# New instruction orders for five queues of a hybrid attention and DeltaNet layer, with the small float32 products of a blockwise inverse in uncut blocks

## The chip, the cores and the metric

The kernel runs on one core of a Trainium2 chip. The metric is the device time of one execution in microseconds (us). A core has five engines that matter here, each with a queue of its own that is executed in order: TensorE (PE in the profile; its weight loads are listed as PEld), VectorE (DVE), ScalarE (ACT), GpSimd (POOL) and SyncE (SP, which issues most of the DMAs). An instruction waits on semaphores of other engines; while it waits, everything behind it in its own queue waits too.

## The reference

The reference is one layer of a diffusion backbone over 512 latent tokens with 256 context tokens, model width 1024, all in float32. A token-mixing half has two branches, softmax attention (8 heads, 2 key/value heads) and a bidirectional gated DeltaNet (8 heads, chunks); their outputs are gated, merged and projected. A channel-mixing half is a gated MLP of width 2816 with a depthwise convolution. The part around which the changed order turns is the triangular solve of the DeltaNet, one unit lower triangular matrix per head, direction and chunk:

```python
a_mat = jnp.where(strict, beta[..., :, None] * dec * kk, 0.0) + jnp.eye(GDN_CHUNK)
rhs = jnp.concatenate([beta[..., None] * v, (beta * jnp.exp(gam))[..., None] * k], axis=-1)
uw = lax.linalg.triangular_solve(a_mat, rhs, left_side=True, lower=True, unit_diagonal=True)
...
delta = u_c - jnp.einsum('bhcd,bhde->bhce', w_c, s)
s_new = gl_c[..., None, None] * s + jnp.einsum('bhcd,bhce->bhde', kd_c, delta)
```

## The kernel before

**Large products.** Every large weight product is done as three products of float32r operands. A weight block of 128x1024 is loaded (`wraw`), ACT rounds it to a high part (`whi`), DVE subtracts to get the low part (`wlo`), and `mm3` multiplies high by high, high by low and low by high into one PSUM bank. In the trace these are the groups of three 128x512 matmuls `mb<-hxH,whi`, `mb<-hxL,whi`, `mb<-hxH,wlo` (the input projections), `pq` (query and key projections), `pS` and `ab` (attention), and `mc` (output projection and MLP).

**Stages.** In order of time: normalisation and modulation, query/key/value projections, attention woven with DeltaNet projections, then the DeltaNet, and from about 789 us on the output projection and the MLP. The DeltaNet goes over four pairs of heads, p = 0 to 3. Through the whole DeltaNet the queue of PE is filled up with the remaining projections (`filler()`), which depend on little, so PE has a large `mb` product at hand while a small chain of the DeltaNet goes through the other engines.

**The solve and the inverse.** Each pair has 12 matrices of 128x128 per direction, made block by block. `gdn_solve` first forms the products of keys (`pk<-kT`), DVE multiplies them into the decay (`NN`), DVE and ACT transpose the diagonal 32x32 blocks (`C`, `X`), and a chain of 31 steps on `R` (`prod`, `R`) inverts all 32x32 diagonal blocks. This chain runs on DVE for pair 0 and on POOL for pairs 1 to 3; for pair p+1 it runs while PE works on pair p. DVE then multiplies `R` by `gT` and transposes it twice, into `o_tr` and `o_nt`. `gdn_inv` assembles the inverse from there in four steps of small float32 products on PE, with copies out of PSUM between them:

1. 48 products of 32x32, `pb<-o_tr,NN` and `pb<-o_nt,NN`, copied to `Y1` by two DVE and two ACT copies;
2. 48 products of 32x32, `pb<-Y,o_nt` and `pb<-Y,o_tr`, copied into `TTm` by DVE and ACT;
3. 24 products of 64x64, `pb<-TTm,NN`, copied to `Y2_0` and `Y2_1`;
4. 24 products of 64x64, `pb<-Y,Tm` (`Y_0`, `Y_1` in the queue's rows), copied into `TTm` by ACT.

The products of a step use parts of the 128x128 array, four different 32x32 parts or two different 64x64 parts by turns, as the loop of the first step shows:

```python
for u in range(12):
    for (d, a, b), py in zip(AB, pys):
        mm(py[q(a), u, :], NN[q(b), u, q(a)], TT[d][q(b), 12 * d + u, :])
```

A float32 product is two records in the trace, a transpose and a float32r product one. After `gdn_inv` follows `gdn_scan`, six steps of 128x128 float32 products (`pb<-S,kT`, `pb<-r,TTm`, `pb<-dk,ktok` and others) that hand over to DVE and ACT in between.

**What sets the order.** All instructions are recorded by wrappers around the five engines, in the order of the program text. At the end `arrange` puts each engine's instructions into the order of a string of numbers, `V_ORDER` (DVE), `A_ORDER` (ACT), `G_ORDER` (POOL), `S_ORDER` (SP) and `T_ORDER` (PE). A number is the instruction's place in the program text, and "260-265" is a run of them. Only the places change; what waits for what follows from the data. Because the recording is a helper, nearly all instructions carry one line, L301 before and L275 after.

Of the kernel before, what the change touches and what calls it, by code (L numbers as in the profile page):

```python
# [70 lines left out]
V_ORDER = ('2 6 5 0-1 3-4 7-65 70 66 71 75 67 76-77 68 120 78 72 79-80 69 82 73 83-84 81 91 85-86 92 74 87-88 90 '  # L71
# [218 lines left out]
def hybrid_layer_body(tc, ctxt, xT, consts, cols, rows, w_mod1, w_mod2, w_av, w_aq, w_cm, w_pa, w_pd, w_out,  # L290
# [27 lines left out]
    def keep(i):  # L318
        return i if V_ORDER else tc.keep_in_program_order(i)

# [1641 lines left out]
```

## Time and profile before

| What | Value |
|---|---|
| median of 3 runs | 1210.79 us (1210.16 to 1213.17) |
| the profiled execution, its own time | 1211.39 us |
| its span | 1209.6 us |
| mean granted clock of TensorE | 0.996 |
| PE busy | 1187.7 us, 98% of the span, 7781 records |
| DVE busy | 819.9 us, 68% |
| ACT busy | 589.1 us, 49% |
| POOL busy | 254.4 us, 21% |

The table of busy time says which engine has no room; the chain of waits says what released each step. PE has under 22 us in which it does nothing, spread over the whole span, so what its instructions cost in themselves is of interest, and a busy PE can still be a PE that is slow. The timeline gives for each group of equal matmuls the start, the length and the number of records. Neighbouring matmuls overlap, so a matmul's cost is read from the step between two starts and not from its length.

### The profile page before, as it was taken

The numbers are of one execution on the slowest core, as the hardware profiler recorded it, in microseconds if no ns is written. First come the engines' busy times: TensorE is split into PE (matmuls) and PEld (weight loads), VectorE is DVE, ScalarE is ACT, GpSimd is POOL, SyncE is SP. The second block draws the span as 40 slices with busy tenths as digits, with TensorE's granted clock in tenths as the row PEclk, the third lists the DMA queues.
The fourth block names the chain that finished last, engine by engine and source line by source line (L and its number), as shares of the span: only waits on it lengthen the run. The fifth ranks groups of instructions, "written<-read, shape, count | busy, mean of one in ns | idle before, by whom it ended". The sixth has DMA issues, their size and how long they took to land.

```text
span 1209.6 us, 20365 instructions
## 1 busy us (share of the span) xinstructions
PE 1187.7 (98%) x7781; PEld 1018.6 (84%) x7781; DVE 819.9 (68%) x1614; ACT 589.1 (49%) x1372; POOL 254.4 (21%) x333
## 2 busy tenths in 40 slices
PE   9999999999998999999999999999999999999996
PEld 6899999999886887888887787889888888888886
DVE  4768788787798667857566798657767656643233
ACT  3535588776656755834535432233444434442221
POOL 0201110101324795785474111000000000000000
PEclk9999999999999999999999999999999999999999
DMA  9423233313453426345245778753432333333331
GB/s 380 161 85 117 94 106 109 103 55 133 172 204 124 153 85 212 125 130 193 93 164 198 257 244 311 238 193 105 170 126 88 105 101 100 98 93 96 96 96 70
DMA packets 57633, 174.96 MB, mean 145 GB/s; under 512 B 6240, under 2 KB 8768, under 8 KB 56128
## 3 DMA queue, kind: packets, MB, share of 16 engines
q1 hardware_dynamic: 54080, 161.08, 39.4%
q0 software_dynamic: 3456, 12.58, 3.1%
q8 instruction: 61, 1.00, 0.4%
q14 instruction: 36, 0.29, 0.1%
HBM read 146.85 MB, written 26.79 MB: 144 GB/s over the span
## 4 chain that ended last, share of the span: by engine, by line
PE 86%; DVE 6%; issue 4%; DMA 2%; ACT 1%; POOL 1%; POOLq 0%; SPq 0%; DVEq 0%; ACTq 0%
PE mc L301 34%; PE mb L301 25%; PE pb L301 8%; PE pq L301 7%; PE ab L301 5%; PE pS L301 3%; PE pm L301 1%; PE xb L301 1%; DVE R L301 1%; PE pk L301 1%; DVE wlo L301 1%; PE pt L301 1%; DVE t L301 1%; DVE prod L301 1%; DMA NN<-nnd 1%
## 5 line engine op out<-in xcount | busy, mean ns | idle before, releaser
L301 ACT ACTIVATE whi<-wraw 128x1024 fp32r<-128x1024 f32 (+3 forms) x155 | 159.4, 1031 | 204.8 <-PE mc L301 110.3
L301 DVE TENSOR_TENSOR wlo<-wraw,whi 128x1024 fp32r<-128x1024 f32 (+3 forms) x155 | 187.0, 1209 | 97.7 <-ACT whi L301 97.5
L301 PE MATMUL mc<-h,whi 128*128 128x512 f32 (+1 forms) x752 | 219.4, 376 | 0.0
L301 PE MATMUL mb<-hxH,whi 128*128 128x512 f32 x384 | 164.4, 428 | 3.3 <-DVE t L301 1.6
L301 PEld LDWEIGHTS mc<-h,whi 128*128 128x128 f32 x752 | 138.0, 188 | 25.4
L301 PE MATMUL mb<-hxH,wlo 128*128 128x512 f32 x384 | 151.9, 396 | 0.0
L301 PE MATMUL mb<-hxL,whi 128*128 128x512 f32 x384 | 150.0, 394 | 0.0
L301 PE MATMUL mc<-h,wlo 128*128 128x512 f32 (+1 forms) x376 | 141.2, 375 | 0.0
L301 PE MATMUL mc<-a,whi 128*128 128x512 f32 (+1 forms) x396 | 111.0, 366 | 0.6 <-DVE x L301 0.6
L301 POOL TENSOR_TENSOR rc<-rc,mhalf 128x2 f32<-128x2 f32 x4 | 2.8, 700 | 441.7 <-DVE rc L301 441.7
L301 PEld LDWEIGHTS mb<-hxH,whi 128*128 128x128 f32 x384 | 72.7, 189 | 18.6 <-ACT hxH L301 2.0
L301 DVE SCALAR_TENSOR_TENSOR u<-mc,col,u 128x511 f32<-128x511 f32 x88 | 64.4, 746 | 34.0 <-ACT u L301 33.3
L301 PEld LDWEIGHTS mb<-hxH,wlo 128*128 128x128 f32 x384 | 72.5, 189 | 16.3
L301 PEld LDWEIGHTS mc<-a,whi 128*128 128x128 f32 x396 | 71.6, 189 | 12.9 <-DVE x L301 0.8
L301 PEld LDWEIGHTS mc<-h,wlo 128*128 128x128 f32 x376 | 70.8, 188 | 12.9
L301 PEld LDWEIGHTS mb<-hxL,whi 128*128 128x128 f32 x384 | 72.8, 190 | 9.9 <-DVE hxL L301 0.5
L301 PE MATMUL mc<-a,wlo 128*128 128x512 f32 (+1 forms) x198 | 72.3, 365 | 0.0
L301 POOL TENSOR_TENSOR R<-R,prod 128x31 f32<-128x31 f32 (+15 forms) x93 | 57.8, 622 | 6.7
L301 POOL TENSOR_TENSOR prod<-X,R 128x31 f32<-128x31 f32 (+15 forms) x93 | 52.5, 565 | 24.3 <-DVE X L301 17.4
L301 DVE SCALAR_TENSOR_TENSOR t<-mb,col,t 128x511 f32<-128x511 f32 (+1 forms) x76 | 49.1, 646 | 12.2 <-ACT t L301 11.4
L301 PE MATMUL pq<-whi,hxH 128*128 128x256 f32 (+1 forms) x192 | 55.7, 290 | 0.0
L301 PE MATMUL pq<-wlo,hxH 128*128 128x256 f32 (+1 forms) x192 | 54.5, 284 | 0.1
(322 smaller groups left out, 2746.7 us busy)
## 6 DMA issues: line engine op xcount, KB each, us to landing
wraw<-in_w_cm_dram SPq DMA_DIRECT2D x48, 512.0 KB, 3.8
wraw<-in_w_up_dram SPq DMA_DIRECT2D x44, 512.0 KB, 3.3
wl<-in_w_mod_dram POOLq DMA_DIRECT2D x24, 512.0 KB, 4.9
wm<-in_w_mod_dram SPq DMA_DIRECT2D x8, 1024.0 KB, 13.8
wraw<-in_w_down_dram SPq DMA_DIRECT2D x16, 512.0 KB, 3.5
wraw<-in_w_aq_dram SPq DMA_DIRECT2D x10, 512.0 KB, 3.5
M<-gamdr SPq DMA_DIRECT2D x8, 512.0 KB, 6.4
wraw<-in_w_pa_dram SPq DMA_DIRECT2D x8, 512.0 KB, 3.7
```

The source lines that it names most:

```text
L301: self.made.append(fn(*a, **k))
```

## The change

The five strings are written anew; `S_ORDER` has the same numbers as before. On DVE 1171 of 1582 instructions stand at another place, on ACT 866 of 1182, on POOL 104 of 329 and on PE 4103 of 6638. The mean move is 2.0 places on DVE, 2.5 on ACT, 0.9 on POOL and 5.6 on PE; the largest is 58 places, on PE. Nothing is added, and nothing is removed: the same 6638 matmuls with the same shapes are there. The diff is the tables alone:

```diff
-T_ORDER = ('0-244 260-265 245-247 266-268 248-259 269-359 362-370 360-361 371-382 386-396 383-385 397-444 '
+T_ORDER = ('0-244 260-262 245-259 263-304 308-315 305-307 316-321 334-335 322-333 336-361 386-387 362-385 '
...
-           '2932 2936 2940 2944 2948 2952 2929 2933 2937 2941 2945 2949 2953 2930 2934 2938 2942 2946 2950 2931 '
...
+           '2920-2927 2976-2997 2928-2975 3048-3053 2998-3047 3054-3065 3070-3072 3066-3069 3085-3088 3073-3084 '
```

The small products of `gdn_inv` are the numbers that stood singly or in strides of four, as 2932, 2936, 2940; they now stand as runs in the order of the program text, as 2928-2975. Counted over the whole PE queue, a piece being a stretch of 32x32 or of 64x64 products with nothing else in between, there were 18 pieces of 32x32 products and 30 of 64x64, and now there are 8 and 9. Within the pieces a product was followed by one on the same part of the array 85 times (32x32) and 87 times (64x64); now never.

Three places show it. The first is PE in the third step of pair 1. Before:

```order
L301 MATMUL pb<-TTm,NN 64x64 x11
L301 MATMUL pk<-kT 128x128 x4
L301 MATMUL mb<-hxH,whi 128x512
L301 MATMUL mb<-hxL,whi 128x512
L301 MATMUL mb<-hxH,wlo 128x512
L301 MATMUL pb<-TTm,NN 64x64 x3
L301 MATMUL mb<-hxH,whi 128x512
L301 MATMUL mb<-hxL,whi 128x512
L301 MATMUL mb<-hxH,wlo 128x512
L301 MATMUL pb<-TTm,NN 64x64 x10
```

Now:

```order
L275 MATMUL xb<-cst,co 128x128 x4
L275 MATMUL pk<-kT 128x128 x4
L275 MATMUL pb<-TTm,NN 64x64 x24
L275 MATMUL mb<-hxH,whi 128x512
L275 MATMUL mb<-hxL,whi 128x512
L275 MATMUL mb<-hxH,wlo 128x512
```

The 24 products of the step stood in three pieces with two groups of large products and the key products of the next pair between them; they are one piece, and the key products stand ahead of it.

The second place is PE between the first and the second step of pair 1, where the second step needs the copies `Y1` of what the first one made. Before:

```order
L301 MATMUL pb<-o_nt,NN 32x32
L301 MATMUL pk<-kT 128x128 x4
L301 MATMUL pb<-o_tr,NN 32x32 x2
L301 MATMUL mb<-hxH,whi 128x512
L301 MATMUL mb<-hxL,whi 128x512
L301 MATMUL mb<-hxH,wlo 128x512
L301 MATMUL mb<-hxH,whi 128x512
L301 MATMUL mb<-hxL,whi 128x512
L301 MATMUL mb<-hxH,wlo 128x512
L301 MATMUL pb<-Y_3884,o_nt 32x32 x2
```

Now:

```order
L275 MATMUL pb<-o_tr,NN 32x32
L275 MATMUL pb<-o_nt,NN 32x32
L275 MATMUL mb<-hxH,whi 128x512
L275 MATMUL mb<-hxL,whi 128x512
L275 MATMUL mb<-hxH,wlo 128x512
L275 MATMUL mb<-hxH,whi 128x512
L275 MATMUL mb<-hxL,whi 128x512
L275 MATMUL mb<-hxH,wlo 128x512
L275 MATMUL pb<-Y_3884,o_nt 32x32
L275 MATMUL pb<-Y_3884,o_tr 32x32
```

Six large products stand between the steps in both. Before, all but the last three products of the first step stood further ahead, so most of its four banks were complete earlier; now all four banks are complete only with the end of the piece.

The third place is DVE at the same point, with the buffer numbers kept (`pb_5750` and `pb_5752` are two of the first step's four banks). Before:

```order
L301 STREAM_TRANSPOSE o_nt_5670<-R_4958 128x32x32
L301 TENSOR_TENSOR oacc_5292<-oacc_5292,pb_5693 128x2x128
L301 SCALAR_TENSOR_TENSOR t1_5618<-mb_5619,col_74,t1_5618 128x511 x2
L301 TENSOR_TENSOR wlo_6023<-wraw_6021,whi_6022 128x1024
L301 SCALAR_TENSOR_TENSOR co_5611<-co_5611,t1_5618 128x512
L301 COPY Y1_3884<-pb_5752 32x384
L301 COPY Y1_3884<-pb_5750 32x384
```

Now:

```order
L275 STREAM_TRANSPOSE o_nt_5670<-R_4958 128x32x32
L275 TENSOR_TENSOR oacc_5292<-oacc_5292,pb_5687 128x2x128
L275 STREAM_TRANSPOSE gT_6820<-g_6819 128x32
L275 TENSOR_TENSOR wlo_6023<-wraw_6021,whi_6022 128x1024
L275 COPY Y1_3884<-pb_5750 32x384
L275 TENSOR_TENSOR f_6281<-f_6281,oss_6264 128x8
L275 COPY Y1_3884<-pb_5752 32x384
```

The convolution steps `t1` and `co` have left the stretch between the transpose `o_nt` and the two copies; one weight split `wlo` still stands ahead of the copies.

More of the change, by code (lines that the diff above doesn't have):

```diff
@@ L68 @@
 AQ, AK, AM, AR = 24, 10, 32, 10
-V_ORDER = ('2 6 5 0-1 3-4 7-65 70 66 71 75 67 76-77 68 120 78 72 79-80 69 82 73 83-84 81 91 85-86 92 74 87-88 90 '
[61 rows of a table removed]
-A_ORDER = ('0-32 34 33 36-37 68 39-40 54 35 41-44 46 45 47 38 49 48 50 55 52 56-57 53 58 51 59-62 64-65 63 69-71 '
[44 rows of a table removed]
-G_ORDER = ('0-9 11 10 12-22 24 28 26 23 29 25 27 33 30 35 34 36-37 31 123 39 38 40 117 41 118 32 42 46 48 43 49 '
[4 rows of a table removed]
+V_ORDER = ('2 6 5 0-1 3-4 7-65 70 66 71 67-68 72 75-76 78 77 73 79-80 82 74 83-84 81 120 69 85 92 86 91 87 93 89 '
[61 rows of a table added]
+A_ORDER = ('0-32 34 33 36-37 68 39-40 35 41-42 54 38 43-44 46 45 47-50 55 51-53 56 58 57 60 59 61 64-65 63 62 67 '
[43 rows of a table added]
+G_ORDER = ('0-9 11-12 10 13-14 16 15 17-20 22 24 28 25-27 30 29 21 32 35 23 33 36 123 37 31 34 41 39 117-118 46 '
[4 rows of a table added]
 S_ORDER = ('0-18 21 24 22-23 25-26 19-20 27-32 34-36 38 41 33 47 54 42 44 37 39 57 40 49-50 52 63 43 45 58-59 61 '
```

366 rows, old and new, of tables (A_ORDER, G_ORDER, T_ORDER, V_ORDER) are left out of this document.

## The prediction

> **What bounds the kernel now.** I read the busy times first, then the chain of waits, then the busy times by stretches, and last the timeline of PE where the order changes. The page's busy row and chain row:
>
> ```profile
> span 1209.6 us, 20365 instructions
> PE 1187.7 (98%) x7781; PEld 1018.6 (84%) x7781; DVE 819.9 (68%) x1614; ACT 589.1 (49%) x1372; POOL 254.4 (21%) x333
> PE 86%; DVE 6%; issue 4%; DMA 2%; ACT 1%; POOL 1%; POOLq 0%; SPq 0%; DVEq 0%; ACTq 0%
> ```
>
> PE is busy for 98% of the span and holds 86% of the chain that ended last. It can get faster in two ways: by the 22 us in which it idles, or by instructions that take less of its time. Busy times by stretch (start and end, length, then the busy time of each engine with its records, the granted clock, DMA share and GB/s) show where it idles:
>
> ```profile
> 300.00:374.00 74.00, 69.56 (x395) 59.56 (x394) 63.90 (x122) 42.47 (x111) 22.42 (x16) 0.98 0.46 167
> 374.00:404.00 30.00, 30.00 (x392) 23.28 (x391) 22.19 (x35) 22.31 (x52) 10.63 (x13) 1.00 0.49 164
> 675.00:735.00 60.00, 58.10 (x355) 50.75 (x354) 52.72 (x116) 19.90 (x45) 8.08 (x16) 1.00 0.79 265
> 789.00:1190.00 401.00, 400.42 (x1949) 338.97 (x1948) 223.94 (x319) 156.84 (x225) 1.41 (x2) 1.00 0.34 111
> ```
>
> From 789 us on PE lacks 0.6 us of 401; no order of the same products can win there. In the first blockwise inverse, 374 to 404, it does not idle at all, so only the price of its instructions counts. That price is the first thing the change touches.
>
> **The price of a cut.** In the timeline (start, length, engine, operation, records), pair 1, third step, a cut is seen between large products:
>
> ```profile
> 482.96 0.40 PE L301 MATMUL mb<-hxH,wlo 128*128 128x512 f32 x1
> 483.28 0.44 PE L301 MATMUL pb<-TTm,NN 64*64 64x64 f32 x6
> 483.66 0.50 PE L301 MATMUL mb<-hxH,whi 128*128 128x512 f32 x1
> 484.00 0.39 PE L301 MATMUL mb<-hxL,whi 128*128 128x512 f32 x1
> 484.22 0.40 PE L301 MATMUL mb<-hxH,wlo 128*128 128x512 f32 x1
> 484.55 0.80 PE L301 MATMUL pb<-TTm,NN 64*64 64x64 f32 x20
> 485.28 0.51 PE L301 MATMUL mb<-hxH,whi 128*128 128x512 f32 x1
> 485.62 0.40 PE L301 MATMUL mb<-hxL,whi 128*128 128x512 f32 x1
> 485.86 0.39 PE L301 MATMUL mb<-hxH,wlo 128*128 128x512 f32 x1
> ```
>
> A large product alone takes a step of 0.23 us (484.00 to 484.22). From 482.96 to 484.22 are 1.26 us with three large products in them, 0.69; so the piece of three small products (six records) cost 0.57. From 484.22 to 485.86 are 1.64 us, again with three large ones; the piece of ten cost 0.95. Seven more products cost 0.38, or 0.054 each. What does not grow with the number is 0.57 - 0.16 = 0.41 us: the step into the piece is 0.32 where 0.23 is usual, the step out is longer than between small products, and the first large product after it steps 0.34. No wait stands at these rows; each piece pays this whatever it holds. For 32x32:
>
> ```profile
> 375.34 0.40 PE L301 MATMUL mb<-hxH,wlo 128*128 128x512 f32 x1
> 375.66 0.31 PE L301 MATMUL pb<-o_tr,NN 32*32 32x32 f32 x4
> 375.90 0.50 PE L301 MATMUL mb<-hxH,whi 128*128 128x512 f32 x1
> 376.24 0.39 PE L301 MATMUL mb<-hxL,whi 128*128 128x512 f32 x1
> 376.47 0.40 PE L301 MATMUL mb<-hxH,wlo 128*128 128x512 f32 x1
> ```
>
> 1.13 us less 0.69 is 0.44 for two products. Inside a piece a product costs 0.02 to 0.05 (next rows), so the fixed part is about 0.36.
>
> There are 10 fewer pieces of 32x32 (18 to 8) and 21 fewer of 64x64 (30 to 9): 10 x 0.36 + 21 x 0.41 = **12.2 us** saved. The 128x128 float32 products, also moved, I cost at nothing: their number of pieces hardly changes (223 to 213), and the rows show the fixed price at changes of the array's part.
>
> **The price of repeats.** Inside a piece it matters whether a product follows one on the same part of the array. Two pieces of 11 products each, with the instruction after them, then two pieces of 32x32:
>
> ```profile
> 480.66 0.91 PE L301 MATMUL pb<-TTm,NN 64*64 64x64 f32 x22
> 481.50 1.16 PE L301 MATMUL pk<-kT 128*128 128x128 f32 x8
> ...
> 491.88 1.08 PE L301 MATMUL pb<-Y,Tm 64*64 64x64 f32 x22
> 492.88 0.50 PE L301 MATMUL mb<-hxH,whi 128*128 128x512 f32 x1
> ```
> ```profile
> 465.44 0.62 PE L301 MATMUL pb<-o_tr,NN 32*32 32x32 f32 x14
> 467.64 0.50 PE L301 MATMUL mb<-hxH,whi 128*128 128x512 f32 x1
> ...
> 473.67 0.21 PE L301 MATMUL pb<-Y,o_nt 32*32 32x32 f32 x1
> 474.74 0.71 PE L301 MATMUL pk<-kT 128*128 128x128 f32 x4
> ```
>
> The first 64x64 piece has 2 repeats and takes 0.84 us, the second has 7 and takes 1.00: 0.032 a repeat, 87 of them 2.8 us. The 32x32 piece from 465.44 holds 45 products with 23 repeats in 2.20 us, that from 473.67 holds 48 with 5 in 1.07 (0.022 each): up to 0.066 a repeat, but the first had to wait for `o_nt` in its midst (below), so I take less than half, 0.027; 85 of them give 2.3 us (bounds 0 and 5.6). Together **5.1 us**, and with the cuts **17.3 us**, all of it between 374 and 675 us.
>
> **What the new order adds.** Three places have to be priced, since PE now comes earlier to whatever it waits for.
>
> First, the hand-over between steps. All four banks now complete at the end of the piece, so their copies are no longer spread out. Copies of PSUM, minimum, median and maximum in ns:
>
> ```profile
> L301 DVE COPY Y<-pb x16: 550/560/565, 378.6 to 666.3; 32x384 f32<-32x384 f32 x8, 64x384 f32<-64x384 f32 x8
> L301 ACT ACTIVATE Y<-pb x16: 463/482/487, 380.3 to 666.5; 32x384 f32<-32x384 f32 x8, 64x384 f32<-64x384 f32 x8
> ```
>
> Two in a row on DVE are 1.12 us, on ACT 0.96, side by side. Between steps 1 and 2 stand six large products at pairs 1 and 2 (about 1.7 us with the steps in and out), and more at pairs 0 and 3. That covers the copies if DVE is free; it is not when the weight split `wlo` ahead of them runs late. Bounds 0 and 1.6 us a place; I take 0.5 at two places, **+1.0**.
>
> Second, the solve of the next pair. It starts with the last key product `pk` and ends with `o_nt`; these are the last key products and the `o_nt` of pairs 1, 2 and 3:
>
> ```profile
> 394.39 0.71 PE L301 MATMUL pk<-kT 128*128 128x128 f32 x4
> 486.67 0.71 PE L301 MATMUL pk<-kT 128*128 128x128 f32 x4
> 576.58 0.71 PE L301 MATMUL pk<-kT 128*128 128x128 f32 x4
> ```
> ```profile
> 464.10 2.03 DVE L301 STREAM_TRANSPOSE o_nt<-R 128x1024 f32<-128x1024 f32 x1
> 553.32 2.18 DVE L301 STREAM_TRANSPOSE o_nt<-R 128x1024 f32<-128x1024 f32 x1
> 639.47 2.15 DVE L301 STREAM_TRANSPOSE o_nt<-R 128x1024 f32<-128x1024 f32 x1
> ```
>
> End to end the chain takes 466.13 - 395.10 = 71.0 us, 555.50 - 487.38 = 68.1 and 641.62 - 577.29 = 64.3. In the new order PE's own work between the same two points, priced by the steps above (0.23 for a large product, 0.22 for a 128x128 float32 one, half that for a transpose), is 70.2, 69.7 and 67.9 us. So PE arrives 0.8 us early at pair 1 and not early at 2 and 3. This counts on the chain starting with `pk`, which the new order puts some 3, 6 and 7 us nearer to the pair's first step than before. **+0.8**, bounds 0 and 8.
>
> Third, the loads of modulation weights between 660 and 760 us, paced by two buffers at a DMA share of 0.79. They begin when the last projection of `hxH` is done, which moves with PE; PE's work from there to the output projection is 2 us less. Bounds 0 and 2, I take **+0.5**. In the first 374 us the products are the same and PE's order moves little; DVE's last steps of pair 0's solve stand where they stood (`o_nt` has the same DVE work ahead). I take 0, with 3 us either way, since 4.4 us of idle PE stand there.
>
> **The sum.** 1211.4 (the profiled execution's own time) - 12.2 - 5.1 + 1.0 + 0.8 + 0.5 = 1196.4 us. The profiled execution was 0.6 above the median of the runs, so 1195.8, say 1196 us.
>
> **The rivals.** *The solve stays where it is* and becomes the bound. For it: DVE is the queue in front (63.9 of 74 us before pair 0), and an earlier `pk` helps only if DVE takes it up earlier. At pair 1 there was no slack: `o_nt` landed at 466.13 in the midst of the first step. If half of the 3, 6 and 7 us is not taken up, waits of 1.5 + 0.8, 3 - 1.6 and 3.5 - 3.6 us, with the copies late too, come to about 6 us more: 1202; if nothing is taken up, some 11 us: 1207. Against it: POOL, which holds most of the chain, has nothing else to wait for there.
>
> *Slower, by the clock.* A row shows what an idle PE pays on top:
>
> ```profile
> 369.49 0.63 PE L301 MATMUL xb<-cst,co 128*128 128x128 f32 x4 [1.95 <-DVE co L301]
> 371.70 0.63 PE L301 MATMUL mb<-hxH,whi 128*128 128x512 f32 x1
> 372.13 0.63 PE L301 MATMUL mb<-hxL,whi 128*128 128x512 f32 x1
> ```
>
> After 1.95 us of waiting, the large products step 0.43 us in place of 0.23 for some eight products: 1.6 us more. A wait of 2 us at a step of the inverse would cost 3.6. There are 12 hand-overs in the four pairs. From five such waits on the 17.3 us are gone; with seven the time is 1211 - 17 + 25 = 1219. Against it: the hand-overs have 1.7 us and more of products between them, the copies need 1.1. [...]
>
> *Nothing*: the cuts' price is hidden by waits that PE would have had anyway, and comes back as idle time: 1211. Against it stands the stretch 374 to 404, with 30.00 of 30.00 us busy. *More*: the new orders of DVE and ACT also take idle time of PE away before 374 us or after 675: 1190.
>
> **How the numbers follow.** The forecast, with its own range of 1192 to 1201, gets 0.60; more than that 0.12; the solve as bound (1201 to 1207) 0.16; nothing 0.07; slower 0.05. The range runs from 1191 to 1205 and leaves out less than 2 in 10. A measurement of this kernel tells 0.3% (3.6 us) from no change: faster 0.88, same 0.07, slower 0.05.
>
> **What would show it.** In the new profile PE's busy time should fall by 15 to 18 us with its records unchanged, pieces of 48 take about 1.1 us and of 24 about 1.4, and the stretch from the first step of pair 0 to the end of pair 3's inverse be shorter by as much. Idle time of PE before `pb<-o_nt` or `pb<-Y` rows, released by DVE, would show the first rival; steps of 0.43 after them the second. An unchanged PE busy time would make the price of a cut wrong.

## The result and the profile after

The change takes 1202.29 us (median of 6 runs, 1199.31 to 1204.99), against 1208.9 us for the kernel before on the same chip: a ratio of **0.9932** with a 95% interval of 0.9910 to 0.9954. It is faster, by 6.6 us in the medians and 8.2 us by the ratio. The forecast was a gain of about 15 us.

The profiled execution took 1203.08 us. Its page:

```profile
span 1201.3 us, 20365 instructions
PE 1172.9 (98%) x7781; PEld 1012.9 (84%) x7781; DVE 820.8 (68%) x1614; ACT 591.4 (49%) x1372; POOL 257.8 (21%) x333
PE 82%; DVE 9%; DMA 4%; issue 3%; POOL 1%; ACT 1%; SPq 0%; POOLq 0%; DVEq 0%; ACTq 0%
```

PE's busy time fell by 14.8 us (1187.7 to 1172.9) with its 7781 records unchanged. The span fell by 8.3 us only, so PE idles 6.5 us more than before. In the chain that ended last DMA went from 2 to 4% and DVE from 6 to 9%. PE's waits in the change (what waits, for whom, us in total, times, longest):

```profile
PE mb L275 <- DVE ga L275: 4.4, 1, 4.4
PE mb L275 <- DVE t L275: 3.3, 3, 2.9
PE pb L275 <- issue: 2.1, 3, 1.2
PE pt L275 <- DVE QL L275: 0.9, 1, 0.9
PE pb L275 <- DVE o_nt L275: 0.7, 1, 0.7
```

The one wait for `ga` is the largest, and the kernel before has none for `ga`. The stretches that the prediction showed, now:

```profile
300.00:374.00 74.00, 68.94 (x392) 59.28 (x392) 64.67 (x142) 42.49 (x109) 18.49 (x14) 0.98 0.47 171
374.00:404.00 30.00, 29.71 (x417) 24.55 (x416) 24.47 (x39) 23.23 (x55) 13.05 (x16) 1.00 0.53 173
675.00:735.00 60.00, 54.36 (x324) 46.72 (x323) 50.85 (x115) 17.92 (x51) 9.77 (x16) 0.99 0.80 268
789.00:1190.00 401.00, 400.35 (x1982) 340.27 (x1981) 221.08 (x322) 153.96 (x221) 2.28 (x3) 1.00 0.32 103
```

In the first inverse, 374 to 404 us, PE is about as busy as before and does 417 records in place of 392, which fits cheaper small products (the two stretches do not hold quite the same work). From 675 to 735 us it idles 5.6 us, where it idled 1.9.

Two landmarks enclose that late part: SP's issue of the load of `cw`, with which the loads of modulation weights begin, and PE's first product of the output projection, `mc<-y,whi`. Timeline of SP and of PE, before:

```profile
664.52 0.33 SPq L301 DMA_DIRECT2D cw<-in_rows_dram  x1
...
789.12 0.62 PE L301 MATMUL mc<-y,whi 128*128 128x512 f32 x2
```

and in the change:

```profile
651.30 0.33 SPq L275 DMA_DIRECT2D cw<-in_rows_dram  x1
...
780.29 0.61 PE L275 MATMUL mc<-y,whi 128*128 128x512 f32 x2
```

At the first landmark the change is 13.2 us ahead, at the second 8.8. So 4.4 us are lost in the 129 us between them, which took 124.6 before. I call them the late stretch from here on. The experiments ask what the small products cost, and who takes the 4.4 us.

### The profile page after: what moved, and what is told of

It reads as the page before. It is cut to its first block, busy times and chain, and to the rows that moved or that the text cites. A ratio compares the mean times of both kernels' runs of the same rounds, so it can differ in the third digit from the quotient of the medians.

```text
span 1201.3 us, 20365 instructions
## 1 busy us (share of the span) xinstructions
PE 1172.9 (98%) x7781; PEld 1012.9 (84%) x7781; DVE 820.8 (68%) x1614; ACT 591.4 (49%) x1372; POOL 257.8 (21%) x333
## 4 chain that ended last, share of the span: by engine, by line
PE 82%; DVE 9%; DMA 4%; issue 3%; POOL 1%; ACT 1%; SPq 0%; POOLq 0%; DVEq 0%; ACTq 0%
PE mc L275 34%; PE mb L275 24%; PE pb L275 7%; PE pq L275 6%; PE ab L275 4%; PE pS L275 3%; PE pm L275 2%; PE xb L275 1%; DVE R L275 1%; DVE t L275 1%; DMA tdr<-ga 1%; DVE wlo L275 1%; DMA wl<-in_w_mod_dram 1%; DVE prod L275 1%; PE pt L275 1%
## 5 line engine op out<-in xcount | busy, mean ns | idle before, releaser
L275 POOL TENSOR_TENSOR prod<-X,R 128x31 f32<-128x31 f32 (+15 forms) x93 | 55.4, 596 | 21.8 <-DVE f L275 12.7
L275 ACT ACTIVATE u<-mc,col 128x512 f32<-128x512 f32 x44 | 33.7, 772 | 46.5 <-PE mc L275 35.1
L275 POOL TENSOR_TENSOR R<-R,prod 128x31 f32<-128x31 f32 (+15 forms) x93 | 53.7, 577 | 6.9
```

Of the source, the lines that this page charges most:

```text
L275: self.made.append(fn(*a, **k))
```

## The experiments

Medians are in us. The ratio is to the kernel before on the same chip. The last three columns are of each kernel's one profile: when the late stretch begins, how long it lasts, and how long PE waits in it for `ga`.

| kernel | orders in the late stretch | median | ratio, 95% | begins | lasts | for `ga` |
|---|---|---|---|---|---|---|
| before | before | 1208.90 | 1 | 664.5 | 124.6 | 0 |
| the change | change | 1202.29 | 0.9932 (0.9910 to 0.9954) | 651.3 | 129.0 | 4.4 |
| e1_regroup | before, PE regrouped | 1198.38 | 0.9907 (0.9892 to 0.9923) | 651.2 | 124.9 | 0 |
| e2_tail_before | before | 1200.90 | 0.9926 (0.9902 to 0.9951) | 648.2 | 130.2 | 0 |
| e3_recut | change | 1216.12 | 1.0066 (1.0045 to 1.0088) | 667.5 | 130.2 | 5.9 |
| e4_repeats_b | change | 1227.36 | 1.0137 (1.0116 to 1.0159) | 673.0 | 129.4 | 5.8 |
| e5_half_loads | change, half the loads | 1193.89 | 0.9866 (0.9845 to 0.9887) | 647.3 | 122.1 | 2.3 |
| e6_half_loads_before | before, half the loads | 1205.79 | 0.9958 (0.9943 to 0.9973) | 663.1 | 121.3 | 0 |
| e7_handover | change | 1202.06 | 0.9938 (0.9921 to 0.9954) | 651.3 | 127.4 | 5.5 |
| e8_head_before | change | 1200.23 | 0.9927 (0.9913 to 0.9941) | 646.7 | 127.7 | 4.3 |
| e9_all_queues | e1, some moved | 1199.56 | 0.9912 (0.9899 to 0.9924) | 647.0 | 128.6 | 1.9 |
| e10_all_half | e9, half the loads | 1189.98 | 0.9833 (0.9819 to 0.9847) | 650.2 | 119.1 | 0 |
| e11_gate_first | change, 2 of DVE moved | 1204.50 | 0.9941 (0.9921 to 0.9961) | 650.8 | 130.3 | 4.4 |
| e12_gate_late | e1, 2 of DVE moved | 1202.38 | 0.9926 (0.9912 to 0.9941) | 650.2 | 127.4 | 0 |

The column "begins" has to be read with care. The change and e5 are the same kernel up to the first load of `wl` (the modulation weights), and their profiles have it at 650.83 and 647.25 us; for e9 and e10 it is 643.46 and 646.69. So two executions of the same instructions can come to this place 3 to 4 us apart, and a difference of that size in the column shows nothing. How much the length of the stretch varies from one execution to the next was not measured by itself. The six kernels with the change's orders in it and full loads (e11 with two moves) lie between 127.4 and 130.3 us, the two with the orders of before throughout at 124.6 and 124.9.

### Regrouping alone

```diff
 # T_ORDER; V, A, G and S as before
-... 2924-2928 2932 2936 2940 2944 2948 2952 2929 2933 2937 2941 2945 2949 2953 2930 ... 2958 2960 2959 2962 ...
+... 2924-2975 2980-2991 2976-2979 2992-3053 ...
```

> Kernel before, with the queues of DVE, ACT, POOL and SP left as they were; on PE alone the 48 pieces of small products of the inverse are gathered into the 17 uncut blocks of the changed kernel, each at the place of its middle product. Theory (a cut costs 0.36 to 0.41 us, a repeat about 0.03, and the gain that is missing after the change was lost in waits that the other queues' new orders brought): PE's busy time falls by 15 to 17 us, PE's added waits stay below 4 us, and the time is 1193 to 1197 us. Rival 1 (the late stretch is paced by the loads of the modulation weights, whatever the order): PE's busy time falls as much, but the waits grow by 7 to 9 us and the time is 1200 to 1203. Rival 2 (the gain came from the new order of the other products and engines, not from the cuts): PE's busy time falls by less than 5 us and the time is 1205 to 1209.

With PE's small products in uncut blocks, and everything else as before, the ratio is 0.9907. That is at least the whole of the change's gain; the two intervals overlap, so better than the change is not shown. The median, 1198.4, is above the 1193 to 1197 that were expected, and PE's busy time fell by 14.5 us, where 15 to 17 were. No kernel with the whole work did better than this one. PE's busy time is that of the change (the busy row of the page, span 1197.1 us):

```profile
PE 1173.2 (98%) x7781; PEld 1011.7 (85%) x7781; DVE 819.9 (68%) x1614; ACT 589.8 (49%) x1372; POOL 254.3 (21%) x333
```

So all of the cheaper small products come from the grouping on PE. The new orders of DVE, ACT and POOL, and the other moves on PE (e1 moves 575 of PE's instructions, the change 4103), brought nothing that can be measured. The two profiled executions can be compared closely, since both begin the late stretch at the same time. The late stretch of this kernel, then of the change (length, PE's busy time and the rest as above):

```profile
651.16:776.10 124.94, 120.09 (x682) 98.95 (x681) 99.44 (x201) 43.88 (x91) 15.21 (x26) 1.00 0.77 259
```
```profile
651.30:780.29 128.99, 121.55 (x682) 101.12 (x681) 99.29 (x199) 43.02 (x89) 15.54 (x26) 0.97 0.75 251
```

With 682 records in each, the change takes 4.05 us longer: 2.6 us more idle time and 1.5 us more of busy time at a granted clock of 0.97. The two executions took 1198.89 and 1203.08 us, 4.2 us apart. In these two executions the difference lies wholly in that stretch.

### The price of a cut

```diff
 # T_ORDER
-2988-2997 2928-2975 3048-3053 2998-3047 ...
+2988-2997 2928-2943 3048-3050 2944-2959 3051-3053 2960-2975 2998-3013 3054-3056 ...
```

> Changed kernel, with its 17 blocks cut again: one or two trios of large products that stand right behind a block are put inside it, at its thirds. 31 more pieces (14 of 32x32, 17 of 64x64), everything else in place, so each block ends at most 1.4 us of large products later. Theory: 14 x 0.36 + 17 x 0.41 = 12 us more of PE's busy time, and 1212 to 1216 us. Rival (a cut costs little; the price read from the rows was a wait that happened to lie there): 1202 to 1205 us.

Each block is cut at its thirds, with the large products that followed it put into the cuts. The third step of pair 1 in the change:

```profile
476.90 1.61 PE L275 MATMUL pb<-TTm,NN 64*64 64x64 f32 x48
478.44 0.50 PE L275 MATMUL mb<-hxH,whi 128*128 128x512 f32 x1
...
482.00 0.61 PE L275 MATMUL pk<-kT 128*128 128x128 f32 x4
```

and cut:

```profile
486.35 0.68 PE L294 MATMUL pb<-TTm,NN 64*64 64x64 f32 x16
...
487.86 0.68 PE L294 MATMUL pb<-TTm,NN 64*64 64x64 f32 x16
...
489.36 0.68 PE L294 MATMUL pb<-TTm,NN 64*64 64x64 f32 x16
...
492.15 0.60 PE L294 MATMUL pk<-kT 128*128 128x128 f32 x4
```

Both rows of starts enclose the same 24 small and 15 large products, without a wait. They take 5.10 and 5.80 us, so a cut of 64x64 products costs **0.35 us** (forecast 0.41). The blocks of 32x32, read in the same way, give 0.32 (forecast 0.36). At these prices the kernel's 14 more cuts of 32x32 and 16 more of 64x64 (the expectation counted 17) come to 10 us. It lost 13.8 us in the medians and 16 by the ratios. Its profiled execution (1220.66 us, above the median) shows where the rest can go: from 374 us to the late stretch PE's busy time is 13.2 us more than in the change and its idle time 3.0, since each block now ends later and the second steps wait for their copies (`Y`, up to 1.4 us), with slower products behind those of pair 1 (large ones step 0.43 us from 481.92 us on, and the granted clock from 465 to 555 us is 0.96, where the change has 1.00). So the price of a cut is shown, and the forecast's way of reading it from steps was right to 0.06 us; some 4 to 6 us of the whole loss are not the cuts themselves.

### The price of repeats

```diff
 # T_ORDER
-2988-2997 2928-2975 3048-3053 ...
+2988-2997 2928-2931 2935 2939 2943 2947 2951 2955 2959 2963 2967 2971 2975 2934 2938 ... 2972 3048-3053 ...
```

> Changed kernel, the products inside each of the 17 blocks sorted: after the first product of each bank come all products of one part of the array, then all of the next. 328 repeats of 32x32 and 151 of 64x64 in place of none; no cut added, and no other instruction moved. Theory: 328 x 0.027 + 151 x 0.032 = 13.7 us more, 1214 to 1218 us. Upper bound of the price (0.066 for 32x32): 26 us more, 1228. Rival (a repeat costs nothing; the slower pieces were waits): 1202 to 1204 us.

The blocks stay whole, but within a block the products are sorted by the part of the array that they use. (A first order of this kind, e4_repeats, has no time: in it the queues wait for one another for ever.) The same block as above, and the large product behind it:

```profile
483.57 2.60 PE L315 MATMUL pb<-TTm,NN 64*64 64x64 f32 x48
486.11 0.50 PE L315 MATMUL mb<-hxH,whi 128*128 128x512 f32 x1
```

Start to start it is 2.54 us; in the change it was 1.54 (476.90 to 478.44). The 19 repeats cost 0.052 us each (the other whole blocks of 64x64 take 2.53 or 2.54 us). A block of 32x32 products of pair 3, its first product and the large one behind it, in the change:

```profile
636.64 0.21 PE L275 MATMUL pb<-o_tr,NN 32*32 32x32 f32 x1
...
637.59 0.51 PE L275 MATMUL mb<-hxH,whi 128*128 128x512 f32 x1
```

and sorted:

```profile
653.25 0.21 PE L315 MATMUL pb<-o_tr,NN 32*32 32x32 f32 x1
...
655.93 0.51 PE L315 MATMUL mb<-hxH,whi 128*128 128x512 f32 x1
```

2.68 us in place of 0.95, so 41 repeats cost 0.042 each. Over the kernel's 328 and 151 added repeats these prices give 21.6 us; the medians lie 25.1 apart and PE's busy times 24.7, far above the 13.7 us of the expectation and close to its upper bound of 26. Repeats are dear, here more so than the forecast's 0.027 and 0.032.

### More work between the hand-overs

```diff
 # T_ORDER, pair 1 (pair 2 alike)
-2928-2975 3048-3053 2998-3047 3054-3065 ...
+2928-2975 3048-3059 2998-3047 3060-3065 ...
```

> Changed kernel; at pairs 1 and 2 two more trios of large products (1.4 us of PE's work, taken from right behind the second step's block) stand between the first and the second step's block, 12 in place of 6 products. Nothing else is moved. Theory (PE's waits for the copies, 0.8 us at pair 1 and 1.4 at pair 2, are lost time): they go, and the time falls by 1.5 to 2 us, to 1200.5. Rival (PE gets to its next late operand earlier by as much and waits there instead): the two waits go, the total of PE's idle time stays within 0.7 us, 1202 to 1203 us.

Twelve large products stand between steps 1 and 2 of pairs 1 and 2, in place of six. The waits there are gone, and the time is the same: 0.9938 against 0.9932. PE came no earlier to the late stretch (651.34), waited 5.5 us for `ga` in it, and idles 28.9 us in all (28.4 in the change). This is what the rival in the expectation foresaw: the waits of 0.6 and 1.2 us at these hand-overs were not time by themselves, since PE then waits for the next late operand.

### The head and the tail of the order before

```diff
 # e2_tail_before: V, A, G, T of the change up to a place in the last inverse, of before behind it (T at the joint)
-4223-4226 4233-4235 4229-4232 4236-4242 ...
+4223-4226 4229-4242 ...
 # e8_head_before: of before up to V 682, A 480, G 55, T 2411 instructions, of the change behind it
```

> Changed kernel up to the end of the last inverse (about 683 us in its profile); behind that point PE, DVE, ACT and POOL go on in the order of the kernel before. No small product stands behind that point. Theory (the 4.4 us wait for the bank at 734 us and the slow steps behind it come from the new order of the late stretch): wait and slow steps are gone, 1195 to 1198 us. Rival (PE is early there and waits for the transfers of the modulation weights and of the token sums in any order): a wait of 4 us or more in 690 to 760 us stays, 1200 to 1203 us.

> Kernel before up to the end of pair 0's solve (about 365 us on PE, no small product stands ahead of it), the changed kernel's orders behind that. Theory (the new orders lose some 2 us of PE's time in the first 370 us, in the waits at 112, 323 and 369 us of its profile): 1199.5 to 1201 us. Rival (an earlier PE only waits longer at the next late operand): 1202 to 1203 us.

With the tail of before there is no wait for `ga`. But at the joint stands a wait of 4.5 us for `at`, behind a store and a load of 6.5 and 5.8 us, and the time (1200.9) is that of the expectation's rival. One wait was replaced by another, at the joint of the two orders and not at the old place, so this run does not decide. It fits with a wait for `ga` that belongs to the change's orders, but doesn't show it.

With the head of before PE comes 4.6 us earlier to the late stretch (646.70), which is little more than two executions of the same instructions differ by. It waits 4.3 us for `ga` there. The median of 1200.23 lies in the range that the expectation gave to its theory: by the medians alone (0.9920 of the kernel before on its chip, 0.9945 for the change) e8 is 3 us better. By the ratios with their intervals, 0.9927 against 0.9932, the two cannot be told apart. So whether the change loses time in the first 374 us stays open.

### Half of the loads

```diff
-                G.dma_start(wl, w_mod2[j])
-                keep(V.scalar_tensor_tensor(out=wl, in0=wl, scalar=0.5, in1=cw, ...
+                G.dma_start(wl[:, D // 2:D], w_mod2[j][:, D // 2:D])
+                two = lambda z: z.rearrange("p (a b) -> p a b", b=2)
+                keep(V.scalar_tensor_tensor(out=two(wl[:, :]), in0=wl[:, D // 2:D].unsqueeze(2).to_broadcast([P, D // 2, 2]),
+                                            scalar=0.5, in1=two(cw[:, :]), ...
```

> Changed kernel, but each of the 24 loads of a modulation weight row block on POOL's queue brings only its second half (256 KB in place of 512); DVE's product reads that half twice, at the same width, so the engines keep their work and only the modulation factors change. Left out: half of those weights. Theory (PE's waits between 655 and 740 us come from transfers that are slow because these loads share the DMA engines at a share of 0.8): store and load of the token sums land sooner, the 4.4 us wait and the slow steps behind it go, 1194 to 1198 us. Rival (PE waits there because of the order of DVE's and SP's queues, whatever the traffic): 1200 to 1204 us.

> Kernel before with the same halved loads (same part of the weights left out). Theory (transfers bind the late stretch only once PE comes there earlier): PE idles there for some 5 us before the change, little of which can go: 1206 to 1209 us, so that the gap between this run and the changed kernel with halved loads is 10 us or more in place of 7. Rival (both kernels wait for the loads alike): 1202 to 1204, the gap stays at 7.

These kernels leave out half of the modulation weights. The edit is worth 5 us to the kernel before (0.9958) and 8 us to the change (0.9932 to 0.9866). With the full loads the change is 8 us ahead of the order before, with half of them 11 (12 in the medians). That is 3 us more, but the intervals of the three ratios leave some 4 us either way, so the times alone do not show it. The profiles point the same way: in the change the stretch falls from 129.0 to 122.1 us, by 6.9, with the wait for `ga` at 2.3; before it falls from 124.6 to 121.3, by 3.3. That the order of the change needs the transfers more is thus likely, and not more. The wait for `ga` is shorter with light loads but not gone, so the loads are not all of it. A third buffer for `wl`, which might loosen the loads without leaving any out, was not tried.

### Waits taken out of e1 by small moves in all queues

```diff
 # e9_all_queues, against e1; one of at least 105 moves, V_ORDER (e10_all_half: this and the half loads)
-44-60
+44-46 49 47 50 48 51-60
```

> The first experiment's kernel (orders of before, uncut blocks on PE), with further instructions on DVE, ACT, POOL, SP and PE moved by a few places, so that what PE waits for between 30 and 790 us is issued earlier; SP's queue, which the change leaves as it is, included. Same pieces on PE (18 in place of 17), no instruction added or taken away. Theory (PE's waits behind the regrouping are a matter of the order of the queues, transfers' issues too): PE's idle time falls from 24 to 14 us or less and the time is 1185 to 1191 us. Rival (the waits are the transfers' own time and come back elsewhere): idle time stays above 20 us, 1196 to 1200 us.

> The kernel with all queues moved a little (it reached the last projections of hxH about 5 us before the changed kernel and was still no faster than the regrouping alone), with the 24 loads of modulation weights halved as in the run before (half of these weights left out). Theory (with full loads the transfers set the end of the stretch from 640 to 770 us, and swallow what PE gains ahead of it): with light loads these 5 us come through, 1187 to 1190 us, 4 us or more under the changed kernel with halved loads (1193.9). Rival (the new places of the moved instructions lose it in that stretch themselves): 1193 to 1196 us.

In its profile e9 reaches the late stretch 4.2 us earlier than e1 and its end 0.5 us earlier; the ratio of 0.9912 is that of e1, and PE's idle time, 24.4 us, did not fall. The expected 1185 to 1191 us were missed by far; the rival had this time. With half of the loads the stretch of this kernel falls by 9.5 us, to 119.1, and the time by 9.6, into the range that the theory of the transfers gave. This does not show that the transfers took back a gain of PE: e10 has the same orders and comes to the stretch at 650.2, hardly earlier than e1, so the 4.2 us may be the chance of one execution. And e1 with half of the loads, against which e10 would have to be held, was not run. What is shown is that the full loads cost this order about 10 us. Whether its own moves on DVE within the stretch add to that was not separated.

### Two gate products of DVE

What makes `ga` late can be followed in the queues. `ga` goes from DVE to DRAM and back (`tdr<-ga`, `ga<-tdr`), in a chain of stores and loads on SP. In SP's queue, loads of `sz` stand between them. Such a load needs its buffer free, and that comes with DVE's gate product `g_s` or `g_n`, which reads the old `sz`. In the order of the change DVE does multiplications of `wl` (1.2 us each) ahead of these products; in the order before they stand behind them.

```diff
 # e11_gate_first, against the change: V_ORDER (1107 and 1102 are the two g_s)
-1165 1131 1137 1140 1148 ... 1149-1151 1107 1152 1147 1170 1183 1175 1154 1159 1102 1155
+1165 1107 1131 1137 1140 1148 ... 1149-1152 1147 1102 1170 1183 1175 1154 1159 1155
 # e12_gate_late, against e1: V_ORDER
-1136 1107 1131 ... 1149-1151 1146 1152 1183 1147 1102 1154 1170 1159 1175 1155
+1136 1131 ... 1149-1151 1107 1146 1152 1183 1147 1154 1170 1159 1175 1102 1155
```

> The change, with two instructions of DVE moved forward: the two gate products g_s of the late stretch stand right behind wlo and right behind M, as they do in the order before, in place of behind two and three multiplications of wl. All other orders are those of the change. Theory: the 4.4 us wait of PE for ga and the slow steps behind it (together about 4 us of the stretch from the first load of cw to the first product of the output projection, 129.0 us in the change and 124.9 in the kernel with the products regrouped alone, which starts that stretch at the same time) come from these two places, since SP's chain of stores and loads of ga waits for g_s. The store that was issued at 709.92 us comes 3 us earlier, the wait falls below 1.5 us, the stretch to 125 to 126.5 us, and the median to 1198 to 1200 us. Rival one, the transfers: whatever the order, the loads end the stretch when PE comes early; the wait goes elsewhere, the stretch stays at 128 to 130 us and the median at 1201 to 1203. Rival two, the order of PE or ACT is the cause: the same numbers as rival one, with the wait for ga still there and the store 3 us earlier.

> The kernel with the products regrouped alone (all other orders those of before), with the same two instructions of DVE moved back to where the change has them: the gate products g_s behind the multiplications of wl. Theory (these two places are the cause): a wait of PE for ga of 3 to 5 us appears, the stretch from the first load of cw to the first product of the output projection goes from 124.9 to 127.5 to 129.5 us, and the median from 1198.4 to 1201 to 1203 us. Rivals (the transfers, or the order of PE or ACT): no wait over 1.5 us appears, the stretch stays within 1 us of 124.9, the median at 1197 to 1200.

The stores of `ga` on SP, in the change:

```profile
709.92 0.43 SPq L275 DMA_DIRECT2D tdr<-ga  x1
...
716.71 0.39 SPq L275 DMA_DIRECT2D tdr<-ga  x1
```

in e1:

```profile
706.38 0.42 SPq L290 DMA_DIRECT2D tdr<-ga  x1
...
710.93 0.41 SPq L290 DMA_DIRECT2D tdr<-ga  x1
```

and with the two products moved forward in the change:

```profile
704.55 0.66 SPq L278 DMA_DIRECT2D tdr<-ga  x1
...
716.49 0.32 SPq L278 DMA_DIRECT2D sz<-szd  x1
716.91 0.38 SPq L278 DMA_DIRECT2D tdr<-ga  x1
```

The first store comes 5.4 us earlier, more than the expected 3. The second stays where it was: the load of `sz` ahead of it is issued at 716.49 only. DVE shows why; first this kernel, then e1:

```profile
715.77 0.69 DVE L278 TENSOR_TENSOR g_n<-sz,g_s 128x512 fp32r<-128x512 f32 x1
```
```profile
709.37 0.68 DVE L290 TENSOR_TENSOR g_n<-sz,g_s 128x512 fp32r<-128x512 f32 x1
```

The next gate product, `g_n`, still stands behind two more multiplications of `wl`, the second of which itself waited 2.1 us for its load, and comes 6.4 us later than in e1. The wait for `ga` is 4.4 us as before, the stretch 130.3, the median 1204.5. As a remedy these two moves failed. By the numbers this is what the expectation gave to its second rival, the order of PE or ACT: the store is earlier and the wait is still there. The late `g_n` offers another reason, but this run does not exclude that rival. The other direction went nearly as expected. In e1 with the two products moved back, the same product of PE has a new wait (named for `f`, a short instruction right behind a `ga` in DVE's queue):

```profile
732.94 1.19 PE L290 MATMUL mb<-g_s,whi 128*128 128x512 f32 x2 [2.65 <-DVE f L290]
```

Its stretch goes from 124.9 to 127.4, and its median from 1198.4 to 1202.4. The wait is a little under the expected 3 to 5 us, but the rivals of this run had none over 1.5. By the ratios the loss is 2 us with intervals that overlap, so the one profile carries this verdict more than the times do. DVE's order at the gate products can thus make the late stretch longer by more than half of what the change lost. Whether it is all of it would need a version of the change with both `g_n` moved as well, which was not tried.

## Why the prediction was right, and where it was wrong

The direction and the range (1191 to 1205) held; the forecast of 1196 was 6 us too low. By its steps:

**The cuts**, priced at 12.2 us. Measured prices of 0.32 and 0.35 us give 10 x 0.32 + 21 x 0.35 = 10.6. Right, 1.6 us too high. Why the steps before the change gave 0.41 and 0.36 stays open; the two pieces from which the 0.41 was read hold no repeats.

**The repeats**, priced at 5.1 us. The sorted blocks gave 0.042 and 0.052 us each, which makes 85 x 0.042 + 87 x 0.052 = 8.1. But those are long rows of repeats, and the repeats of the order before stood mostly in shorter ones. With the measured cuts, the two prices of repeats give 15.7 and 18.7 us in all. PE's busy time fell by 14.5 us in e1 and by 14.8 in the change, where it would be 16.3 without the 1.5 us at the lower clock in the late stretch. So the forecast's lower price describes the order before the better, and its "15 to 18 us" of busy time was nearly right, for e1 a little high. Blocks of 48 take 0.95 us and blocks of 24 1.54, where about 1.1 and 1.4 were forecast.

**The hand-overs and the solve**, priced at +1.0 and +0.8. Busy times up to 374 us and from there to the late stretch, before:

```profile
0.00:374.00 374.00, 366.86 (x2518) 326.86 (x2519) 293.56 (x689) 225.78 (x617) 53.36 (x50) 1.00 0.40 140
374.00:664.52 290.52, 288.66 (x2557) 243.30 (x2556) 195.40 (x382) 161.28 (x436) 184.32 (x256) 1.00 0.45 152
```

and in the change:

```profile
0.00:374.00 374.00, 365.72 (x2510) 325.74 (x2511) 291.87 (x687) 227.50 (x614) 53.78 (x47) 1.00 0.39 140
374.00:651.30 277.30, 274.10 (x2559) 236.49 (x2557) 197.75 (x385) 163.12 (x442) 185.50 (x257) 1.00 0.47 158
```

In the second row PE idles 1.9 us before and 3.2 in the change: +1.3 in place of +1.8. The waits stand about where the forecast put them: for `o_nt` at pair 1 (0.7 us) and none at pairs 2 and 3, and within the second steps of pairs 0, 1 and 2 (0.3, 0.6 and 1.2 us, for which the profile names no releaser). e7 shows besides that taking the latter two away is worth nothing here.

**The first 374 us**, taken at 0. PE idles 8.3 us there in place of 7.1. The rows show one wait of 2.92 us for `t` where waits of 1.25 and 1.95 stood. Right within its 3 us in idle time; e8 leaves open whether it cost time.

**The third place, the late stretch**, taken at +0.5 with bounds 0 and 2, is the step that failed: the loss was 4.05 us against e1, the same work begun at the same time, and 4.4 against the kernel before. With the 1.1 and 1.3 us above, PE's added idle time of 4.0 us there makes up the 6.5 us. The rows of the change where it is paid:

```profile
734.66 1.19 PE L275 MATMUL mb<-g_s,whi 128*128 128x512 f32 x2 [4.41 <-DVE ga L275]
...
736.93 0.63 PE L275 MATMUL mb<-g_s,wlo 128*128 128x512 f32 x1
737.36 0.63 PE L275 MATMUL mb<-g_s,whi 128*128 128x512 f32 x1
```

The forecast treated the stretch as PE's remaining work paced by loads, with an order that was as good as before. It looked at when PE comes to it, and not at the order of DVE within it. PE's earlier arrival does not explain it: with the orders of the change, kernels that begin the stretch at 646.7, 651.3, 667.5 and 673.0 us take 127.7, 129.0, 130.2 and 129.4 and wait 4.3 to 5.9 us for `ga`; with those of before, beginnings at 664.5 and 651.2 take 124.6 and 124.9 and have no such wait (e2, which begins at 648.2, takes 130.2 with the 4.5 us at its joint). The chain of waits in the change shows the links: a store, a weight load (whose block ACT and DVE then split), a store and a load, of some 5 us each (start, length):

```profile
709.92 5.15 DMA tdr<-ga
...
715.45 5.55 DMA wraw<-in_w_pd_dram
...
723.32 5.02 DMA tdr<-ga
...
728.35 5.36 DMA ga<-tdr
...
734.66 2.47 PE mb L275 x5
```

A gate product that is late on DVE can move all of it, as in e12 (its store is issued at 708.08 us, that of e1 at 706.38), and with half of the loads the link was shorter: the median store of `ga` takes 5.1 us in the change, at a DMA share of 0.75 in the stretch, and 4.4 there, at 0.67, where the wait was 2.3 us. That DVE's order suffices for a loss of this kind is shown by e12, in one profile; that it is the only cause in the change is not, and the two moves of e11 did not undo the loss.

**The rivals.** *The solve as bound* has the measured time in its range (1201 to 1207), but not for its reason: PE waited 0.7 us in all for `o_nt`. *Slower, by the clock* happened in small: the wait at 734.66 was followed by steps of 0.43 us (736.93 to 737.36 and around) at a granted clock of 0.61 from 734.60 to 742.00 us, which is enough for the 1.5 us of busy time lost in the late stretch. The runs go with it: the six of the change have granted clocks of 0.990 to 0.996, the two slowest (1204.8 and 1205.0 us) the lowest and the fastest (1199.3) the highest, while e1's six have 0.995 to 0.998. *Nothing* and *more* did not occur; the gain is there, and the other queues' new orders gave nothing. The chance of 0.88 for faster was on the right side. That the time fell into the range in spite of the late stretch is owed in part to the width of the range.

## What to carry to other kernels

In these kernels small float32 products that change the array's part cost by the piece (0.32 to 0.35 us a cut) and by the repeat (0.042 to 0.052 us in long rows); both can be read from the starts of two pieces in a timeline, and one grouped order on PE brought all of the gain that was measured here. When a whole schedule is new, price each stage's order by itself: what PE saves early can be lost again in a later stage, for instance where a short instruction that frees a buffer for a DMA now stands behind long ones (in e12 0.69 us behind 1.22). To see which, compare two kernels that begin the stage at the same time, and follow SP's issues back to the engine that each waited for. Before trusting a landmark of one profile to a few us, compare two profiles of kernels that are alike up to it.

## What was not expected of the hardware

The clock after a wait does not follow from the wait's length alone. The same wait at the same place, in the change, in e3_recut and in e4_repeats_b, with the product behind it:

```profile
368.72 0.80 PE L275 MATMUL mb<-hxH,whi 128*128 128x512 f32 x1 [2.92 <-DVE t L275]
369.31 0.63 PE L275 MATMUL mb<-hxL,whi 128*128 128x512 f32 x1
```
```profile
368.53 0.79 PE L294 MATMUL mb<-hxH,whi 128*128 128x512 f32 x1 [2.87 <-DVE t L294]
```
```profile
367.56 0.51 PE L315 MATMUL mb<-hxH,whi 128*128 128x512 f32 x1 [2.91 <-DVE t L315]
367.90 0.40 PE L315 MATMUL mb<-hxL,whi 128*128 128x512 f32 x1
```

After 2.92 us the first step is 0.59 us and the next ones 0.43; after 2.91 us they are 0.34 and 0.23. After the shorter wait of 2.87 us the products are slow again (0.59 us, then 0.43), so a limit on the wait's length does not sort the three. The granted clock from 370 to 373 us is 0.72 in the change, 0.70 in e3_recut and 1.00 in e4_repeats_b. Slow products need not follow at once either: in the kernel before, the four large products from 369.87 us on, behind the wait of 1.95 us, still step 0.32 and 0.23 us, and the steps are 0.40 to 0.43 from 370.88 on only. What counts beside the length is not shown here.

The link of SP's chain is not a fixed price either: 256 KB from `ga` to DRAM took 5.15 us at 709.92 in the change, where the load behind it was issued at 715.09. In e1 the load stood behind its store by 3.2 us (706.38 to 709.57) at nearly the same DMA share of the stretch (0.77 against 0.75), and behind the next store there it stood by 8.0 us (710.93 to 718.97).
